# PEER gather kernel: v rows of token block 0 gathered by token and summed on TensorE, in turn with the u rows of block 1

## The chip, the cores and the metric

One core of one Trainium2 chip runs the whole program. The metric is the device time of one execution in microseconds, as the median of several runs. A profiled execution is one such run with the hardware profiler on; its trace gives the start and end of every instruction, and the span from the first to the last instruction.

## The reference

One layer of an encoder on 1024 tokens of width 1024: RMSNorm, a projection, differential attention (4 heads) beside spatial gating (4 groups), an output projection with a residual, then the PEER step below with a residual, and a last RMSNorm. PEER scores each token against two sets of 128 keys for each of 8 heads, keeps 16 experts of 16384 for each head, and sums their v rows with gated weights:

```python
def peer(xn, w_q, sub_keys, w_u, w_v):
    ...
    def block(xb):                       # 128 tokens
        q = (xb @ w_q).reshape(PEER_TOKEN_BLOCK, PEER_HEADS, 2, PEER_HALF)
        s = jnp.einsum('thpd,hpnd->thpn', q, sub_keys).astype(jnp.float32)
        vals, idx = lax.top_k(s, K)
        ...
        expert = i1 * PEER_KEYS + i2
        g = jax.nn.softmax(best, axis=-1)
        h = jnp.einsum('thkd,td->thk', w_u[expert], xb)
        a = (g * jax.nn.gelu(h.astype(jnp.float32))).astype(xb.dtype)
        return jnp.einsum('thk,thkd->td', a, w_v[expert])
```

So each token has 8 x 16 = 128 pairs; a pair needs one row of `w_u` (1024 floats, 4 KB) for a dot product with the token, and one row of `w_v` to be added with weight `a`.

## The kernel before

The 1024 tokens are 8 blocks of 128. The program has a front (`front()`), in which attention, gating, projections and the choice of experts run in four passes of two blocks each, and after it the PEER sums, done in two ways:

- **Dense blocks** (2 to 5, `dense()`): TensorE goes over all 16384 experts in 128 steps. Each step streams 128 u columns and 128 v rows (512 KB each) through the SP queue, ScalarE and VectorE split them into high and low parts (`uh`, `ul`, `vh`, `vl`, lines 760 to 779), and TensorE does `hp` (lines 765 to 767) and the products into `y` and `op` (lines 743 to 745). The gates `gg` that say which token uses which expert are made in the front by `gates()` from one-hot products (`oh`, `pgg`, `st`; lines 598 to 652) and go through the DRAM array `gd`.
- **Gather blocks** (0, 1, 6, 7): `gather_u(b)` fetches, for each of the 128 pairs j, one u row for each of the 128 tokens, by an indirect DMA on GpSimd's queue (line 664, 128 rows of 4 KB, 512 KB), and VectorE forms the dot product (line 685). `gather_v(b)` fetches v rows in the same way, and VectorE adds each with its weight to `y` (line 699). That is 1024 indirect DMAs in all, named `u` and `v` in the trace. They land in a ring of `GAT` = 5 buffers (pool `gat`); once the front has closed its pools, the gathers in `MIXED` have `GAT2` = 3 more.

The order in which the program is written is `PLAN` for the front, then `SEQ`. Letters: A projection, B attention, M gating, Y and D output projection and residual, S scores and top-16 per key set, t the choice of experts (`select`), u and v gathers, G1 and G2 the gates of blocks 2, 3 and 4, 5. A scheduler then orders each engine's instructions by a timing of its own: an instruction goes where its operands and buffers are free, earlier text having priority, and a tile of a pool waits for its turn at the pool's buffers. On the chip each engine runs its own list in that order. So `u1` and `v0`, which stand behind `d` (dense) in `SEQ`, were in fact placed among the front's instructions: they need only `gat` buffers, GpSimd and VectorE.

PSUM has 8 banks. In the front, pool `accp` has 4, `smp` 3 (attention, transposes, G2's gates) and `vpsp` 1 (the gates of G1, alone). `dense()` takes all 8, six for `kept` and two for `hp`.

The call of G1's gates, and the SEQ loop:

```python
                elif w == "G1":
                    gates(G1B, vpsp, "vps", G1)
...
        for w in SEQ.split():
            if w == "d":
                dense()
            else:
                (gather_u if w[0] == "u" else gather_v)(int(w[1:]))
```

Of the kernel before, what the change touches and what calls it, by code (L numbers as in the profile page):

```python
# [7 lines left out]
F32 = mybir.dt.float32  # L8
F32R = mybir.dt.float32r
BF16 = mybir.dt.bfloat16  # L10
I32 = mybir.dt.int32
U32 = mybir.dt.uint32
AF = mybir.ActivationFunctionType
ALU = mybir.AluOpType
AX = mybir.AxisListType
PSUM = bass.MemoryType.PSUM
# [26 lines left out]
FRONT_POOL = 1.0  # L43
WS = 3
G1B = (2, 3)
G1 = dict(st=1, o1=2, o2=3, gt=1)
G2 = dict(st=3, o1=4, o2=4, gt=2)
PLAN = "A0:34 A0:01g2 B0 Y0 D0 S0 X t0 u0 t1 A1:34201 A2:20134 M1 B1 Y1 D1 S1 A3:01234 B2 M2 t2 t3 Y2 M3 D2 B3 S2 t4 t5 G1 Y3 Z G2 D3 S3"
SEQ = "d u1 v0 v1 u6 v6 u7 v7"
LATE = {2: 6, 6: 7}  # L50
GAT = 5
GAT2 = 3
# [9 lines left out]
def peer_block(tc, d):  # L62
# [3 lines left out]
    with ExitStack() as ctx:  # L66
# [65 lines left out]

        x1_d = [dram.tile([P, D], F32, name=f"x1_{b}") for b in range(NB)]
        gd = dram.tile([P, NTB, P, TB], F32, name="gd")
        xT_d = dram.tile([P, DC, TD], F32, name="xT_d")
        sel_t = {}
        rs2_t = {}
# [91 lines left out]
        def front():  # L229
# [1 line left out]
            E2 = fs.enter_context  # L231
            accp = E2(tc.tile_pool(name="accp", bufs=4, space=PSUM))
            smp = E2(tc.tile_pool(name="smp", bufs=3, space=PSUM))
            vpsp = E2(tc.tile_pool(name="vpsp", bufs=1, space=PSUM))
            kv = E2(tc.tile_pool(name="kv", bufs=1))
            sm = E2(tc.tile_pool(name="small", bufs=4))
            tpool = E2(tc.tile_pool(name="tp", bufs=2))
            wp = E2(tc.tile_pool(name="wp", bufs=WP))
            f2 = E2(tc.tile_pool(name="f2", bufs=2))
            f4 = E2(tc.tile_pool(name="f4", bufs=X4))  # L240
            space["sel"] = E2(tc.tile_pool(name="f1", bufs=1))

            gmix = col(kv, "g_mix", DC)
# [336 lines left out]
            for w in PLAN.split():  # L580
                if w == "X":
                    wss.close()
                elif w == "Z":
                    att.close()
                elif w == "G1":
                    gates(G1B, vpsp, "vps", G1)
                elif w == "G2":
                    gates([b for b in DENSE if b not in G1B], smp, "smp", G2)
                elif w[0] in "uvt":
                    {"u": gather_u, "v": gather_v, "t": select}[w[0]](int(w[1:]))  # L590
                elif w[0] == "A":
# [65 lines left out]
        def fetch(b, src, ix, nm):  # L657
            k_ = ring[0] % (GAT + GAT2)
            ring[0] += 1
            if f"{src[2]}{b}" in MIXED and k_ >= GAT:  # L660
                t = gat2.tile([P, D], F32, name=f"{nm}", tag="gat2")
            else:
                t = gat.tile([P, D], F32, name=f"{nm}", tag="gat")
            pool.indirect_dma_start(out=t, out_offset=None, in_=d[src],  # L664
                                    in_offset=bass.IndirectOffsetOnAxis(ap=ix, axis=0))
            return t

        G = {}

        def gather_u(b):  # L670

            n = NPAIR
            ef, _, g = sel_t[b]
            idx = gxn.tile([P, n], I32, name=f"idx{b}", tag="idx", bufs=2)
            dve.tensor_copy(idx, ef)
            xn = gxn.tile([P, D], F32, name=f"xn{b}", tag="xn")
            x1 = gat.tile([P, D], F32, name=f"gx1{b}", tag="gat")
            pool.dma_start(x1, x1_d[b])
            gr = gat.tile([P, D], F32, name=f"gr{b}", tag="gat")
            pool.dma_start(gr, d["g_ffn_row"].partition_broadcast(P))  # L680
            dve.scalar_tensor_tensor(xn, x1, rs2_t[b], gr, op0=ALU.mult, op1=ALU.mult)
            h = gxn.tile([P, n], F32, name=f"h{b}", tag="h")
            for j in range(n):
                t = fetch(b, "w_u", idx[:, j:j + 1], f"u{b}_{j}")
                dve.tensor_tensor_reduce(t, t, xn, 1.0, 0.0, ALU.mult, ALU.add, h[:, j:j + 1])  # L685
            a = gxn.tile([P, n], F32, name=f"a{b}", tag="a")
            act.activation(a, h, AF.Gelu_apprx_tanh)
            dve.tensor_tensor(a, a, g, ALU.mult)
            G[b] = a, idx

        def gather_v(b):

            n = NPAIR
            a, idx = G[b]
            y = gxn.tile([P, D], F32, name=f"y{b}", tag="xn")
            pool.dma_start(y, x1_d[b])
            for j in range(n):
                t = fetch(b, "w_v", idx[:, j:j + 1], f"v{b}_{j}")
                dve.scalar_tensor_tensor(y, t, a[:, j:j + 1], y, op0=ALU.mult, op1=ALU.add)  # L699
            ms = smg.tile([P, 2], F32, name=f"msg_{b}", tag="msg")  # L700
            jk = gxn.tile([P, D], BF16, name=f"jk3_{b}", tag="jk", bufs=1)
            act.activation(jk, y, AF.Square, accum_out=ms[:, 0:1])
            r = rsqrt(ms[:, 0:1], 1, 1.0 / D, f"rl{b}", smg)
            gf = gat.tile([P, D], F32, name=f"gf{b}", tag="gat")
# [165 lines left out]
```

## Time and profile before

| | |
|---|---|
| median of 3 runs | 2812.53 us (2807.18 to 2818.32) |
| the profiled execution | 2825.71 us, its span 2823.9 us |
| granted TensorE clock, mean | 0.91 of full speed |
| busy: TensorE, VectorE | 2423.6 us (86%), 2404.8 us (85%) |
| busy: ScalarE, GpSimd | 1000.3 us (35%), 1488.8 us (53%) |
| indirect gathers (software queue) | 545.33 MB, 53.0% of the 16 DMA engines' time |

How to read it: a share is a mean over stages with different limits, so the stages are read one by one, by time windows. A window's line gives the busy time of each engine in it. "Idle before" is the time in which an engine stood still ahead of an instruction, and behind the arrow is what ended that wait. fp32 matmuls leave two records in the trace for each call.

### The profile page before, as it was taken

Reading aid. Unit: us, or ns where it says so; the run is one execution under the profiler, and the core shown is the slowest. Engines: PE = TensorE matmul, PEld = TensorE weight load, DVE = VectorE, ACT = ScalarE, POOL = GpSimd, SP = SyncE. Lnnn points to the kernel's source line nnn. Section 1 sums busy time; section 2 is a strip of 40 time slices with the busy share of each in tenths; the row PEclk is TensorE's granted clock in tenths of the full one; section 3 lists DMA queues with packets and bytes.
Section 4 is the critical chain, followed back from the end, with each engine's and each line's share of the span. In section 5 each row is a group of like instructions: output and inputs, shape, how many; then the busy total and the mean of one; then the engine's idle time right before and its main releaser. Section 6 shows DMA issues by size and latency. Waiting matters only on the chain.

```text
span 2823.9 us, 33571 instructions
## 1 busy us (share of the span) xinstructions
PE 2423.6 (86%) x10764; PEld 1909.5 (68%) x10764; DVE 2404.8 (85%) x5223; ACT 1000.3 (35%) x2063; POOL 1488.8 (53%) x1139
## 2 busy tenths in 40 slices
PE   6789997995569774797999999999999999999930
PEld 5575655753447542695887887888888888888820
DVE  4448867999988999999898887987888978888998
ACT  5553322224553542983323232232232322323300
POOL 5362564356655325321265646655566657655665
PEclk9799998996569777898999999999999999999965
DMA  5266999998899858797699999999999989998998
GB/s 174 59 181 184 343 365 359 337 339 297 299 348 331 295 182 290 264 366 247 214 346 350 352 322 366 354 333 342 328 356 343 342 306 384 349 359 303 331 333 343
DMA packets 316514, 869.56 MB, mean 308 GB/s; under 512 B 26033, under 2 KB 93745, under 8 KB 312241
## 3 DMA queue, kind: packets, MB, share of 16 engines
q0 software_dynamic: 149760, 545.33, 53.0%
q1 hardware_dynamic: 166576, 322.09, 33.2%
q8 instruction: 85, 1.39, 0.2%
q14 instruction: 93, 0.75, 0.1%
HBM read 823.28 MB, written 44.04 MB: 307 GB/s over the span
## 4 chain that ended last, share of the span: by engine, by line
PE 61%; DVE 19%; DMA 10%; issue 5%; ACT 4%; POOL 1%; SPq 0%; DVEq 0%; ACTq 0%; POOLq 0%
PE hp L765 7%; PE hp L767 7%; PE hp L766 7%; PE y L745 6%; PE y L743 6%; PE y L744 6%; PE pq L309 5%; DVE y L699 4%; DVE u L685 4%; DMA u<-in_w_u_dram,idx 3%; PE pgg L650 2%; PE wi L309 2%; PE op L743 2%; PE op L745 2%; PE op L744 2%
## 5 line engine op out<-in xcount | busy, mean ns | idle before, releaser
L664 POOL DMA_INDIRECT v<-in_w_v_dram,idx x512 | 664.9, 1299 | 656.5 <-DVE y L699 321.2
L664 POOL DMA_INDIRECT u<-in_w_u_dram,idx x512 | 700.1, 1367 | 530.7 <-DVE h L685 226.7
L699 DVE SCALAR_TENSOR_TENSOR y<-v,a,y 128x1024 f32<-128x1024 f32 x512 | 656.3, 1282 | 15.8 <-DMA v<-in_w_v_dram,idx 9.0
L685 DVE CUSTOM_DVE_ANT_0 u<-u,xn 128x1024 f32<-128x1024 f32 x512 | 614.2, 1220 | 50.6 <-DMA u<-in_w_u_dram,idx 50.2
L765 PE MATMUL hp<-xh,uh 128*128 128x512 f32 x1024 | 400.0, 391 | 22.0 <-ACT xh L726 15.6
L766 PE MATMUL hp<-xl,uh 128*128 128x512 f32 x1024 | 399.3, 390 | 2.4 <-DVE xl L727 2.4
L767 PE MATMUL hp<-xh,ul 128*128 128x512 f32 x1024 | 399.3, 390 | 0.6 <-DVE ul L761 0.6
L778 ACT ACTIVATE vh<-vr 128x1024 fp32r<-128x1024 f32 x128 | 130.7, 1052 | 510.8 <-PE op L745 481.1
L744 PE MATMUL y<-vl,ah 128*128 128x512 f32 x768 | 298.8, 389 | 0.0
L743 PE MATMUL y<-vh,ah 128*128 128x512 f32 x768 | 298.8, 389 | 0.0
L745 PE MATMUL y<-vh,al 128*128 128x512 f32 x768 | 287.6, 389 | 2.2 <-DVE al L775 2.2
L650 PE MATMUL pgg<-oh,oh 128*128 128x128 f32 x1024 | 190.3, 344 | 102.7 <-ACT st L651 63.9
L650 PEld LDWEIGHTS pgg<-oh,oh 128*128 128x128 f32 x1024 | 170.3, 247 | 132.6 <-ACT st L651 84.0
L765 PEld LDWEIGHTS hp<-xh,uh 128*128 128x128 f32 x1024 | 192.7, 188 | 64.4 <-ACT xh L726 15.8
L766 PEld LDWEIGHTS hp<-xl,uh 128*128 128x128 f32 x1024 | 192.7, 188 | 43.0 <-DVE xl L727 3.1
L767 PEld LDWEIGHTS hp<-xh,ul 128*128 128x128 f32 x1024 | 192.6, 188 | 41.4 <-DVE ul L761 1.4
L760 ACT ACTIVATE uh<-ur 128x1024 fp32r<-128x1024 f32 x128 | 135.1, 1056 | 168.7 <-PE hp L766 149.7
L761 DVE TENSOR_TENSOR ul<-ur,uh 128x1024 fp32r<-128x1024 f32 x128 | 156.3, 1221 | 36.6 <-ACT uh L760 36.5
L309 PE MATMUL pq<-sT,sc 128*128 128x256 f32 x768 | 184.0, 389 | 0.7 <-ACT sT L127 0.7
L779 DVE TENSOR_TENSOR vl<-vr,vh 128x1024 fp32r<-128x1024 f32 x128 | 153.5, 1220 | 16.3 <-ACT vh L778 16.3
L745 PEld LDWEIGHTS y<-vh,al 128*128 128x128 f32 x768 | 144.2, 188 | 33.3 <-DVE al L775 3.5
L309 PEld LDWEIGHTS pq<-sT,sc 128*128 128x128 f32 x768 | 143.8, 195 | 32.8 <-issue 10.7
(440 smaller groups left out, 4117.2 us busy)
## 6 DMA issues: line engine op xcount, KB each, us to landing
ur<-in_w_uT_dram SPq DMA_DIRECT2D x128, 512.0 KB, 6.5
vr<-in_w_v_dram SPq DMA_DIRECT2D x128, 512.0 KB, 6.5
wi<-in_w_in_dram SPq DMA_DIRECT2D x80, 512.0 KB, 5.0
sc<-in_w_q_dram SPq DMA_DIRECT2D x64, 512.0 KB, 6.4
gd<-st SPq DMA_DIRECT2D x32, 1024.0 KB, 7.2
gg<-gd SPq DMA_DIRECT2D x16, 2048.0 KB, 21.8
wo<-in_w_out_dram SPq DMA_DIRECT2D x32, 512.0 KB, 7.0
x<-in_x_dram SPq DMA_DIRECT2D x16, 512.0 KB, 6.5
```

The source lines that it names most:

```text
L309: pe.matmul(ps, s_[i], m_[j], start=first and n == 0, stop=last and n == len(ops) - 1, **kw)
L650: pe.matmul(pg[:, j * P:(j + 1) * P], oh2[:, j, :], oh1[:, j, :], start=True, stop=True)
L664: pool.indirect_dma_start(out=t, out_offset=None, in_=d[src], in_offset=bass.IndirectOffsetOnAxis(ap=ix, axis=0))
L685: dve.tensor_tensor_reduce(t, t, xn, 1.0, 0.0, ALU.mult, ALU.add, h[:, j:j + 1])
L699: dve.scalar_tensor_tensor(y, t, a[:, j:j + 1], y, op0=ALU.mult, op1=ALU.add)
L743: pe.matmul(ps, ah[:, bs], vh[:, hs], start=first, stop=False, skip_group_check=True)
L744: pe.matmul(ps, ah[:, bs], vl[:, hs], start=False, stop=False, skip_group_check=True)
L745: pe.matmul(ps, al[:, bs], vh[:, hs], start=False, stop=last, skip_group_check=True)
L761: dve.tensor_tensor(ul, ur, uh, ALU.subtract)
L765: pe.matmul(hp[:, :TD], uh[:, ds_], xh[:, dc, :], start=(dc == 0), stop=False)
L766: pe.matmul(hp[:, :TD], uh[:, ds_], xl[:, dc, :], start=False, stop=False)
L767: pe.matmul(hp[:, :TD], ul[:, ds_], xh[:, dc, :], start=False, stop=(dc == DC - 1))
```

## The change

Block 0's v sum leaves VectorE. `tokens_v` turns the expert numbers and the weights `a` by a transpose, so that a gather fetches for one token its 128 rows (one pair on each partition). A matmul with a 128x32 weight matrix, zero but for one column that holds the token's `a`, adds the sum over pairs to one row of a PSUM tile; the column moves over 32 places, and the four 32-column groups of the array take two tokens by two halves of the row. Each of 64 steps (2 halves `r`, 32 `j`) has two gathers and four fp32 matmuls of 512 columns. `both` interleaves this with the u rows of block 1, in turn, as the last item `w01` of `PLAN`; `u1` and `v0` leave `SEQ`. G1's gates now share `smp` in place of the bank `vpsp`, which `vyp` takes for the sums, and have one `oh1` buffer fewer.

```diff
-G1 = dict(st=1, o1=2, o2=3, gt=1)
+G1 = dict(st=1, o1=2, o2=2, gt=1)
...
-PLAN = "A0:34 A0:01g2 B0 Y0 D0 S0 X t0 u0 t1 A1:34201 A2:20134 M1 B1 Y1 D1 S1 A3:01234 B2 M2 t2 t3 Y2 M3 D2 B3 S2 t4 t5 G1 Y3 Z G2 D3 S3"
-SEQ = "d u1 v0 v1 u6 v6 u7 v7"
+PLAN = "A0:34 A0:01g2 B0 Y0 D0 S0 X t0 u0 t1 A1:34201 A2:20134 M1 B1 Y1 D1 S1 A3:01234 B2 M2 t2 t3 Y2 M3 D2 B3 S2 t4 t5 G1 Y3 Z G2 D3 S3 w01"
+SEQ = "d v1 u6 v6 u7 v7"
+TENSOR = [0]
+VJ = 1
...
-            vpsp = E2(tc.tile_pool(name="vpsp", bufs=1, space=PSUM))
+            vyp = E2(tc.tile_pool(name="vyp", bufs=1, space=PSUM))
...
+            sv = E2(tc.tile_pool(name="sv", bufs=1))
...
-                    gates(G1B, vpsp, "vps", G1)
+                    gates(G1B, smp, "smp", G1)
...
+                elif w[0] == "w":
+                    both(int(w[1]), int(w[2]), smp, vyp, sv)
...
+        def tokens_v(b, pp, vyp, sv):
...
+            ef = sel_t[b][0]
+            pt = pp.tile([P, 512], F32, name=f"vt{b}", tag="smp")
+            pe.transpose(pt[:, 0:P], ef, ident)
+            pe.transpose(pt[:, P:2 * P], G[b][0], ident)
+            ixT = sv.tile([P, P], I32, name=f"ixT{b}", tag="ixT")
+            aT = sv.tile([P, P], F32, name=f"aT_{b}", tag="aTv")
+            act.activation(ixT, pt[:, 0:P], AF.Copy)
+            act.activation(aT, pt[:, P:2 * P], AF.Copy)
+            W = [sv.tile([P, 2, VJ, 63], F32, name=f"vw{b}_{i}", tag=f"vw{i}") for i in range(2)]
+            for w_ in W:
+                dve.memset(w_, 0.0)
+            for r in range(2):
+                ps = vyp.tile([P, 512], F32, name=f"vy{b}_{r}", tag="vy")
+                for j in range(32):
+                    w_ = W[j // VJ % 2]
+                    if j % VJ == 0:
+                        act.activation(w_[:, :, :, 31], aT[:, r * 64:r * 64 + 64].rearrange("p (g j) -> p g j", g=2)[:, :, j:j + VJ], AF.Copy)
+                    vs = [fetch(b, "w_v", ixT[:, r * 64 + g * 32 + j:r * 64 + g * 32 + j + 1], f"v{b}_{r}_{j}_{g}") for g in range(2)]
+                    for hf in range(2):
+                        for g in range(2):
+                            q0 = 64 * hf + 32 * g
+                            pe.matmul(ps[q0:q0 + 32, :], w_[:, g, j % VJ, 31 - j:63 - j], vs[g][:, hf * 512:(hf + 1) * 512],
+                                      start=(j == 0), stop=(j == 31), tile_position=(0, q0), skip_group_check=True)
+                    yield
+                    yield
+                y2 = gat.tile([P, D], F32, name=f"vs{b}_{r}", tag="gat")[:, 0:512]
...
+                dve.tensor_tensor(y2, y2, ps, ALU.add)
+                for hf in range(2):
+                    pool.dma_start(yv_d[b][r * 64:(r + 1) * 64, hf * 512:(hf + 1) * 512], y2[64 * hf:64 * hf + 64, :])
+            y = gxn.tile([P, D], F32, name=f"y{b}", tag="xn")
+            pool.dma_start(y, yv_d[b])
+            finish_v(b, y)
...
+        def both(bv, bu, pp, vyp, sv):
...
+            todo = [rows_u(bu), tokens_v(bv, pp, vyp, sv)]
+            while todo:
+                for g_ in list(todo):
+                    if next(g_, 0) == 0:
+                        todo.remove(g_)
```

`rows_u` is the old `gather_u` with a `yield` behind each row, and `finish_v` the old end of `gather_v` (the last norm and the store of the block).

What the scheduler made of it shows in the lists of the engines. Three places follow.

TensorE, the gates of block 2 (`gt2` are their transposes, `pgg` their products; `ops5` and `ops7` are the attention sums of blocks 5 and 7). Before:

```order
L477 MATMUL ops5_4810<-v4_174,aT5_3_4_4941 128x128
L477 MATMUL ops5_4810<-v5_175,aT5_3_4_4941 128x128
L611 MATMUL gt2_1_6559<-ident_75,rj2_5148 128x128
L611 MATMUL gt2_2_6562<-ident_75,g2_5153 128x128
L650 MATMUL pgg0_0_6576<-oh1_0_0_6568,oh2_0_0_6567 128x128 x4
L650 MATMUL pgg0_4_6591<-oh1_0_4_6583,oh2_0_4_6582 128x128 x4
```

Now:

```order
L481 MATMUL ops7_5753<-v7_181,aT7_3_4_5898 128x128
L125 MATMUL mT7ap0_5931<-ident_75,mix7_5751 128x128
L617 MATMUL gt2_0_6560<-ident_75,ri2_5144 128x128
L125 MATMUL mT7ap0_5931<-ident_75,mix7_5751 128x128 x3
L617 MATMUL gt2_1_6563<-ident_75,rj2_5152 128x128
L617 MATMUL gt2_2_6566<-ident_75,g2_5157 128x128
L313 MATMUL wo3_0_7_8622<-wo3_0_0_8623,mT3_5485 128x512 x2
L313 MATMUL wo3_0_7_8622<-wo3_0_1_8629,mT3_5485 128x512 x2
L656 MATMUL pgg0_0_6580<-oh1_0_0_6572,oh2_0_0_6571 128x128 x4
```

The gates of blocks 2 and 3 stood between the attention of block 5 and that of block 6; now they stand behind the attention of block 7, the last one.

TensorE, the end of the front (`ss` are the last scores, `hp` the first products of the dense stage). Before:

```order
L559 MATMUL ss6_3_9100<-kt3_3_8995,sq3_3_9039 128x128 x2
L559 MATMUL ss7_3_9129<-kt3_3_8995,sq3_3_9039 128x128 x2
L765 MATMUL hp0_9229<-xh_9189,uh0_9225 128x512
L765 MATMUL hp1_9271<-xh_9189,uh1_9267 128x512
L766 MATMUL hp0_9229<-xl_9190,uh0_9225 128x512
```

Now:

```order
L656 MATMUL pgg31_8_8594<-oh1_31_8_8586,oh2_31_8_8585 128x128 x3
L656 MATMUL pgg31_12_8609<-oh1_31_12_8601,oh2_31_12_8600 128x128 x4
L708 MATMUL vt0_9174<-ident_75,ri0_2372 128x128
L709 MATMUL vt0_9174<-ident_75,a0_2786 128x128
L727 MATMUL vy0_0_9185<-v0_0_0_0_9187,vw0_0_9181 32x512
L727 MATMUL vy0_0_9185<-v0_0_0_1_9189,vw0_0_9181 32x512
L727 MATMUL vy0_0_9185<-v0_0_0_0_9187,vw0_0_9181 32x512
L727 MATMUL vy0_0_9185<-v0_0_0_1_9189,vw0_0_9181 32x512
L727 MATMUL vy0_0_9185<-v0_0_1_0_9202,vw0_1_9182 32x512
```

and 250 matmuls further on:

```order
L727 MATMUL vy0_1_9672<-v0_1_31_0_10139,vw0_1_9182 32x512
L727 MATMUL vy0_1_9672<-v0_1_31_1_10141,vw0_1_9182 32x512
L828 MATMUL hp0_10255<-xh_10215,uh0_10251 128x512
L828 MATMUL hp1_10297<-xh_10215,uh1_10293 128x512
L829 MATMUL hp0_10255<-xl_10216,uh0_10251 128x512
```

All 256 matmuls of the new sum (`vy`) stand in a row, behind the last gate and ahead of the first `hp`.

GpSimd, behind the last u row of block 0 (`dio` is the index row for the gates of G2). Before:

```order
L664 DMA u0_127_2779<-in_w_u_dram,idx0_2389 128x1024
L678 DMA gx11_18114<-x1_1_87 128x1024
L680 DMA gr1_18116<-in_g_ffn_row_dram 128x1024
L664 DMA u1_0_18120<-in_w_u_dram,idx1_18111 128x1024
L664 DMA u1_1_18123<-in_w_u_dram,idx1_18111 128x1024
L664 DMA u1_2_18126<-in_w_u_dram,idx1_18111 128x1024
```

The rest of `u1` follows there in a row, and `v0` behind it.

Now:

```order
L670 DMA u0_127_2783<-in_w_u_dram,idx0_2393 128x1024
L684 DMA gx11_9165<-x1_1_87 128x1024
L686 DMA gr1_9167<-in_g_ffn_row_dram 128x1024
L670 DMA u1_0_9171<-in_w_u_dram,idx1_9162 128x1024
L610 IOTA dio_7598 128x128
L670 DMA v0_0_0_0_9187<-in_w_v_dram,ixT0_9177 128x1024
L670 DMA v0_0_0_1_9189<-in_w_v_dram,ixT0_9177 128x1024
L670 DMA u1_1_9195<-in_w_u_dram,idx1_9162 128x1024
L670 DMA u1_2_9198<-in_w_u_dram,idx1_9162 128x1024
L670 DMA v0_0_1_0_9202<-in_w_v_dram,ixT0_9177 128x1024
```

Behind the first u row of block 1 GpSimd now has the index row of G2 and two v rows that need the transposed indices `ixT`; the rest alternates, two u rows and two v rows.

## Rows read from the trace of the kernel before

**Rows 1.** The page: span, busy time of each engine and its share of the span.

```profile
span 2823.9 us, 33571 instructions
PE 2423.6 (86%) x10764; PEld 1909.5 (68%) x10764; DVE 2404.8 (85%) x5223; ACT 1000.3 (35%) x2063; POOL 1488.8 (53%) x1139
```

**Rows 2.** Time windows (start:end, length, then busy us of each engine, clock, DMA, GB/s).

```profile
core 0: us, PE busy (x) PEld busy (x) DVE busy (x) ACT busy (x) POOL busy (x), PEclk, DMA share, GB/s
560.00:650.00 90.00, 87.24 (x296) 51.06 (x295) 90.00 (x368) 20.93 (x45) 49.10 (x39) 0.98 0.94 331
650.00:1085.00 435.00, 288.99 (x1239) 215.08 (x1239) 400.15 (x1140) 196.95 (x542) 218.72 (x176) 0.72 0.83 291
1085.00:1297.00 212.00, 168.52 (x921) 139.75 (x920) 205.65 (x597) 144.01 (x379) 68.16 (x54) 0.89 0.89 311
1297.00:2707.00 1410.00, 1398.32 (x6144) 1153.24 (x6143) 1224.06 (x1642) 409.91 (x527) 813.22 (x577) 1.00 0.92 331
960.00:1040.00 80.00, 62.83 (x249) 43.14 (x249) 72.58 (x236) 43.66 (x109) 19.75 (x21) 0.69 0.64 211
```

**Rows 3.** All gathers of u and of v: duration min/median/max ns, first and last start.

```profile
L664 POOL DMA_INDIRECT u<-in_w_u_dram,idx x512: 932/1346/4157, 270.7 to 2566.9; - x171
L664 POOL DMA_INDIRECT v<-in_w_v_dram,idx x512: 932/1020/3759, 852.6 to 2805.8; - x171
```

**Rows 4.** Dense matmuls: `hp` first start, `op` last start, the page's line on `hp`.

```profile
L765 PE MATMUL hp<-xh,uh x1024: 387/389/792, 1296.6 to 2687.2; 128*128 128x512 f32 x171
L745 PE MATMUL op<-vh,al x256: 388/389/389, 1342.9 to 2706.5; 128*128 128x512 f32 x128
L765 PE MATMUL hp<-xh,uh 128*128 128x512 f32 x1024 | 400.0, 391 | 22.0 <-ACT xh L726 15.6
```

**Rows 5.** VectorE by line, 565 to 1297 us (busy us, mean ns | idle before).

```profile
L699 DVE SCALAR_TENSOR_TENSOR y<-v,a,y 128x1024 f32<-128x1024 f32 x129 | 165.1, 1280 | 2.7 <-DMA v<-in_w_v_dram,idx 2.3
L685 DVE CUSTOM_DVE_ANT_0 u<-u,xn 128x1024 f32<-128x1024 f32 x130 | 156.9, 1218 | 14.8 <-DMA u<-in_w_u_dram,idx 14.8
```

**Rows 6.** TensorE by line, 650 to 1085 us.

```profile
L650 PE MATMUL pgg<-oh,oh 128*128 128x128 f32 x512 | 113.5, 388 | 84.4 <-ACT st L651 62.1 <-DVE oh L641 14.1 <-ACT oh L646 3.7
L309 PE MATMUL pq<-sT,sc 128*128 128x256 f32 x256 | 60.7, 385 | 0.0
```

**Rows 7.** TensorE by line, 1085 to 1297 us.

```profile
L650 PE MATMUL pgg<-oh,oh 128*128 128x128 f32 x512 | 76.8, 300 | 18.4 <-DVE oh L641 8.3 <-ACT oh L645 4.7 <-ACT oh L646 3.5
L309 PE MATMUL pq<-sT,sc 128*128 128x256 f32 x256 | 62.4, 387 | 0.7 <-ACT sT L127 0.7
```

**Rows 8.** ScalarE by line, 565 to 1297 us.

```profile
L646 ACT ACTIVATE oh<-oh,gT 128x128 f32<-128x128 f32 x256 | 111.7, 491 | 11.1 <-DVE gT L613 11.1
L645 ACT ACTIVATE oh<-iota,gT 128x128 f32<-128x128 f32 x256 | 89.1, 402 | 11.8 <-PE pgg L650 11.7
L651 ACT ACTIVATE st<-pgg 128x512 f32<-128x512 f32 x128 | 76.2, 596 | 94.1 <-PE pgg L650 67.0 <-DMA gd<-st 26.9
```

**Rows 9.** Tile `gd`, 960 to 1045 us: gate stores, five of them, issue to landing.

```profile
DMA to landing us min/median/max: 3.8/5.4/7.2
```

**Rows 10.** Tile `v`, 960 to 1040 us: gathers under light DMA load, issue to landing.

```profile
L664 POOL DMA_INDIRECT v<-in_w_v_dram,idx x21: 936/937/1003, 960.9 to 1037.1; - x21
DMA to landing us min/median/max: 4.1/4.6/6.6
```

**Rows 11.** TensorE, fp32 matmuls of 512 columns in a row, 565 to 1297 us.

```profile
L309 PE MATMUL wi<-wi,xT 128*128 128x512 f32 x96 | 43.0, 598 | 0.0
```

**Rows 12.** Timeline of GpSimd in the tail, gathers of v7 alone (start, duration, engine).

```profile
2768.78 1.02 POOL L664 DMA_INDIRECT v<-in_w_v_dram,idx  x1 [0.30 <-issue]
2770.10 1.01 POOL L664 DMA_INDIRECT v<-in_w_v_dram,idx  x1 [0.30 <-issue]
```

**Rows 13.** Gathers of v at the start of the dense stage and 100 us later.

```profile
L664 POOL DMA_INDIRECT v<-in_w_v_dram,idx x14: 936/1138/3759, 1298.2 to 1398.8; - x14
L664 POOL DMA_INDIRECT v<-in_w_v_dram,idx x47: 933/1144/1993, 1400.0 to 1496.1; - x47
```

More of the change, by code (lines that the diff above doesn't have):

```diff
@@ L134, in peer_block @@
         gd = dram.tile([P, NTB, P, TB], F32, name="gd")
+        yv_d = {b: dram.tile([P, D], F32, name=f"yv_{b}") for b in TENSOR}
         xT_d = dram.tile([P, DC, TD], F32, name="xT_d")
@@ L668, in peer_block, with rows_u @@
         G = {}
-        def gather_u(b):
+        def rows_u(b):
             n = NPAIR
@@ L689, in gather_u @@
             G[b] = a, idx
+        def gather_u(b):
+            for _ in rows_u(b):
+                pass
+        def tokens_v(b, pp, vyp, sv):
[23 more added lines that the diff above has]
+                    yield
+                    yield
+                y2 = gat.tile([P, D], F32, name=f"vs{b}_{r}", tag="gat")[:, 0:512]
+                rows = x1_d[b][r * 64:(r + 1) * 64, :]
+                for hf in range(2):
+                    pool.dma_start(y2[64 * hf:64 * hf + 64, :], rows[:, hf * 512:(hf + 1) * 512])
+                dve.tensor_tensor(y2, y2, ps, ALU.add)
+                for hf in range(2):
+                    pool.dma_start(yv_d[b][r * 64:(r + 1) * 64, hf * 512:(hf + 1) * 512], y2[64 * hf:64 * hf + 64, :])
+            y = gxn.tile([P, D], F32, name=f"y{b}", tag="xn")
+            pool.dma_start(y, yv_d[b])
+            finish_v(b, y)
@@ L699, in gather_v, with finish_v @@
                 dve.scalar_tensor_tensor(y, t, a[:, j:j + 1], y, op0=ALU.mult, op1=ALU.add)
+            finish_v(b, y)
+        def finish_v(b, y):
             ms = smg.tile([P, 2], F32, name=f"msg_{b}", tag="msg")
```

## The prediction

> **What bounds the kernel now.** I read the page first: VectorE 85% and TensorE 86% busy over the span, so neither share alone tells the limit [rows 1]. Then time windows, because the stages differ [rows 2]. In the front from 560 to 1297 us VectorE is busy for 90.0 of 90, 400.2 of 435 and 205.7 of 212 us, TensorE for 87.2, 289.0 and 168.5: behind 650 us VectorE is the limit and TensorE's clock falls to 0.72 for want of work. From 1297 to 2707 us TensorE is busy for 1398 of 1410 us at clock 1.00: the dense stage is bound by TensorE, from its first `hp` at 1296.6 to its last `op` at 2706.5 [rows 4]. Then the gathers of block 7 go on alone: the last v gather is issued at 2805.8 [rows 3], and the span ends at 2823.9. So the end is set by the stream of gathers, which runs from 270.7 to 2805.8 without a long break, 1024 of them at a mean of (2805.8 - 270.7) / 1023 = 2.48 us; and the dense stage runs beside it and ends 117 us earlier.
>
> What counts for the change is therefore: when does the dense stage start, and how many gathers are left at that moment. Before, at 1297 us, all of u0, u1 and v0 are done (384 gathers) and 640 are left. After the change the same 384 must be done before the first `hp`, because TensorE's list has all `vy` matmuls ahead of it. From there the same 640 gathers and the same dense work remain. The new time is the new start of the dense stage plus about what follows it now, 2823.9 - 1296.6 = 1527 us.
>
> **Part 1: what leaves VectorE.** The 128 v additions of block 0 (mean 1.28 us) are about 164 us, and 128 u rows of block 1 (1.22 us and a short read of the sum) about 157 us move out of the front's middle to its end [rows 5]. Both were spent in the front, where VectorE was the limit. They are a gain only as far as the front really gets shorter.
>
> **Part 2: the front without them.** GpSimd's list is unchanged up to the first u row of block 1. The 256 u gathers of blocks 0 and 1 lie between 270.7 and the first v at 852.6, 2.27 us each, so the 129th is at about 561 us [rows 3]. Until 650 us TensorE is full (87.2 of 90) and nothing is won. Then the order of the gates decides. Since G1's gates now share `smp`, they wait for their turn behind the attention of block 7. What is left of 650 to 1085 us without gates is TensorE's 289.0 - 113.5 = 176 us [rows 2, 6]; to this I add an estimated 45 us, a quarter, for chains of norm and transpose that nothing fills (in the window behind it TensorE idles 43.5 us beside 168.5 of work [rows 2]): attention ends at about 871 us. G1 then has 16 chunks of 16 tokens with a single `st` buffer. ScalarE needs for one chunk 4 copies of 76.2 / 128 = 0.60 us, 8 first steps of 89.1 / 256 = 0.35 and 8 second steps of 111.7 / 256 = 0.44, in sum 8.7 us [rows 8]; about 2.7 us of it (six one-hot steps) stand in its list ahead of the first copy of the next chunk and so run while the store of the last chunk lands, which takes 3.8 to 7.2, median 5.4 us under light load [rows 9]. A chunk is 5.4 + 6.0 = 11.4 us, 16 of them 182 us (157 to 211). G1 ends at 1053 us. Behind it come the second half of D3, S3 and G2: TensorE has 168.5 us in the window that holds them now, 76.8 of it G2's gates and 62.4 the scores [rows 2, 7], VectorE 205.7 less some 50 for v0. I take 172 us: 1225. The two transposes, the copies to `ixT` and `aT` and the first landing of a v row (4.6) are 8 us more: the first `vy` at 1233 us (1195 to 1275). So the front, up to there, is only some 48 us shorter than its 1281 us now (1296.6 less the wait of 15.6 for `xh` [rows 4]): the 320 us that left VectorE are given back to waits, as the gates were hidden beside attention and the gathers, and now stand alone. GpSimd does next to nothing from 565 to 1225 us: the ring of five is held by `u1_0` to `u1_2` and the first two v rows, which need `ixT`.
>
> **Part 3: the pair of sums.** Now 256 gathers run with five buffers and little beside them. A buffer is used again five gathers later, and four gathers make a step (two u, two v), so the second v row of a step takes the buffer of the first v row of the step before. It cannot be issued until TensorE is done with that row, and TensorE cannot go on until it has landed. The period of a step is that loop: issue to landing 4.6 us under light load (4.1 to 6.6) [rows 10]; then two more matmuls until the first row is free (the first of the four needs only the first row and is done already); then two hand-overs between queues, an estimated 0.6 us (twice the 0.30 that stands between gathers [rows 12]). An fp32 matmul of 512 columns is two records of 43.0 / 96 = 0.45 us, so 0.9 us at a granted clock of 0.98 and 1.8 us at half of it [rows 2, 11]; no row of this trace has a matmul of 32 columns. Bounds for two of them: 0.9 us (side by side, full clock) to 3.6 us (one behind the other, half clock). I take 1.8. The period is 4.6 + 1.8 + 0.6 = 7.0 us, 64 steps 448 us. GpSimd's own pace, 1.32 us from one gather to the next [rows 12], would allow 5.3 us a step, and VectorE's two u rows 2.6 us: both are hidden. I add an estimated 30 us: two periods at the turn from the first half to the second (GpSimd's queue waits for the addition of 64 rows), and a third of the 50 us that the selects of blocks 6 and 7 take (Part 4), since ScalarE's weights stand behind them in its list. TensorE leaves the sums at 1233 + 478 = 1711 us.
>
> The Trainium skill, page "TensorE: Matmul & The Clock Gate", section "Part 3: Packing small matmuls", says that matmuls on different column groups run at the same time, and gives 2.38 times for three tiles of 32 columns and 512 columns of data. By that rule the two matmuls cost 0.9 to 1.8 us, not up to 3.6, and the sum would be that of rival B or mine. No run here shows it yet.
>
> **Part 4: the dense stage and the tail.** `xh` is made behind the last u row, and TensorE waits for it as now: 15 us, so the first `hp` is at 1726 us. Of the 1527 us that follow now, some come back: in the first 100 us GpSimd issues 14 gathers, in the next 47 [rows 13]. The gap of 33 gathers at 2.1 us is 70 us of a VectorE full with the choice of experts for blocks 6 and 7 and the first splits. The selects now run beside the sums, where VectorE has room; I take 50 us back (0 to 70). The end is 1726 + 1477 = 3203 us of span. The profiled execution stands 1.8 us above its span and 13.2 us above the median (2825.71 against 2812.53), so the forecast is 3203 + 1.8 - 13.2 = **3192 us**, 13% slower.
>
> Hidden at no cost: the extra stores and loads of `yv` (they lie beside the first dense products), ScalarE's 64 small copies of weights (a step ahead), the memsets.
>
> **Rivals.**
> - B, quick sums: the matmuls of a step go side by side at full clock, two cost 0.9 us, and the period is 6.1 us or less, down to GpSimd's 5.3. Then the sums take 338 to 390 us instead of 448, and the time is 3082 to 3134. For it: four different column groups. Against: TensorE would be idle for most of a step, and in the window from 960 to 1040 us, with more work than that, the clock was 0.69.
> - C, slow sums: matmuls one behind the other at half clock, a period of 8.8 us, 115 us more: 3307. Or gathers come no faster than u rows did with the same five buffers, 2.27 us each, 581 us instead of 448: 3325. For it: that was the pace in the front. Against: 0.94 busy DMA engines there, which would be much less here.
> - D, faster: the front was bound by VectorE, and shrinks by all of 322 us, to 959; the sums go at GpSimd's pace, 256 x 1.32 = 338 us; dense starts at 959 + 338 + 15 = 1312, the span ends at 1312 + 1477 = 2789, the time is 2778, 1.2% faster. It decides if the sums end before about 1320 us. Against: TensorE alone has 545 us of work from 560 to 1297, and the gates stand behind attention in its list.
> - E, no change: halfway between, the sums end at about 1330 us. It needs nearly all that D needs.
>
> That the change doesn't do what it says is not among them: the additions are gone from VectorE's list.
>
> **How the numbers follow.** Forecast 50%, B 24%, C 21%, D 3%, E 2%. The range reaches over B's lower end with a front at its early bound, and over C: 3060 to 3330 us. About 0.5%, 14 us, is what a measurement can tell from no change: faster 0.03, same 0.02, slower 0.95.
>
> **What would show it.** In the profile after: GpSimd nearly idle from about 565 to 1225 us; the first `vy` at 1195 to 1275; 64 steps of 6 to 9 us, with TensorE waiting for DMA of v and GpSimd waiting for TensorE; the first `hp` right behind the last `vy`; from there to the end some 1480 us, with the tail of block 7 behind TensorE as now. I would be wrong if gates ran well before 871 us, if the gathers of `u1` filled the gap, or if the stage behind the first `hp` were shorter than 1410 us.

## The result, and the profile after

The changed kernel takes 3164.4 us against 2813.5 us: a ratio of 1.1237, with a 95% interval from 1.120 to 1.1275, so 12% slower. One of its four executions was in a slower state (3782.2 us at a granted clock of 0.683); the ratio leaves it out, the median has it in. The profiled execution has a span of 3153.2 us (before 2823.9).

Time windows of the kernel after; columns as in [rows 2].

```profile
560.00:650.00 90.00, 82.35 (x291) 47.28 (x289) 68.13 (x322) 22.86 (x58) 0.37 (x1) 1.00 0.41 125
650.00:880.00 230.00, 194.47 (x771) 127.62 (x771) 146.16 (x718) 82.40 (x241) 0.00 (x0) 0.85 0.28 85
880.00:1085.00 205.00, 163.97 (x936) 137.18 (x936) 116.86 (x307) 185.24 (x505) 0.23 (x1) 0.92 0.41 156
1085.00:1235.00 150.00, 88.75 (x493) 60.23 (x491) 133.73 (x574) 63.19 (x171) 41.66 (x35) 0.76 0.74 259
1235.00:1670.00 435.00, 215.41 (x496) 31.61 (x496) 149.09 (x242) 20.95 (x69) 269.18 (x238) 0.58 0.84 284
1670.00:3060.00 1390.00, 1384.54 (x6095) 1144.70 (x6094) 1195.94 (x1453) 399.35 (x515) 814.24 (x592) 1.00 0.94 339
```

From 650 to 1085 us VectorE, the limit there before, is busy for 263 of 435 us (before 400 [rows 2]), and GpSimd for a quarter of a microsecond. From 1235 to 1670 us there is a stage that the kernel before does not have: TensorE is half busy at a clock of 0.58, and no engine is full (the DMA engines stand at 0.84). Behind it the dense stage is what it was: 1405 us from the first `hp` to the last `op`, before 1410.

The tiles of gates, v sums and dense products in the kernel after: count, duration of one in ns (least, median, most), first and last start in us, shape. They answer to [rows 4, 6, 7].

```profile
L656 PE MATMUL pgg<-oh,oh x1024: 272/275/582, 859.7 to 1145.2; 128*128 128x128 f32 x171
...
L727 PE MATMUL vy<-v,vw x512: 589/1061/1063, 1153.7 to 1650.4; 128*32 128x512 f32 x171
...
L828 PE MATMUL hp<-xh,uh x1024: 389/389/796, 1655.8 to 3040.2; 128*128 128x512 f32 x171
```

The gates run from 860 to 1145 us, behind the attention and no longer beside it; the sums from 1154 to 1651; `hp` follows 4.4 us after the end of the last `vy`. The difference of the spans, 329 us, comes out of these rows: the front up to the first `vy` is 142.9 us shorter than the front up to the first `hp` was (1153.7 against 1296.6), sums and their hand-over add 502.1, and from the first `hp` to the end it takes 1497.4 us instead of 1527.3, which is 29.9 back. About 25 of these lie behind the last `op`, where the remaining gathers take 93 us instead of 117.

GpSimd's list in the kernel after around its long pause (start, us, instruction, and in brackets how long the engine stood idle before it and what ended that).

```profile
559.38 0.99 POOL L670 DMA_INDIRECT u<-in_w_u_dram,idx  x1 [2.03 <-DVE rep L571]
995.62 0.23 POOL L610 IOTA dio<- 128x128 int32 x1 [435.25 <-PE mT7bp L125]
1146.52 0.97 POOL L670 DMA_INDIRECT v<-in_w_v_dram,ixT  x1 [150.67 <-ACT aT L713]
```

GpSimd works through its list in order: the `iota` of G2's gates waits until the last transpose of block 7 is done, and behind it the first v row waits for `aT`, since the sums stand last in `PLAN`. So from 650 to 1085 us, where the DMA engines are busy for only 0.28 to 0.41 of the time, no gather is issued.

### The profile page after: what moved, and what is told of

The parts are those of the page before. It is cut to its first block, busy times and chain, and to the rows that moved or that the text cites. A ratio compares the mean times of both kernels' runs of the same rounds, so it can differ in the third digit from the quotient of the medians.

```text
span 3153.2 us, 34803 instructions
## 1 busy us (share of the span) xinstructions
PE 2614.2 (83%) x11278; PEld 1903.2 (60%) x11278; DVE 2280.0 (72%) x5099; ACT 1002.4 (32%) x2125; POOL 1453.0 (46%) x1147
## 3 DMA queue, kind: packets, MB, share of 16 engines
q1 hardware_dynamic: 166576, 322.09, 29.9%
## 4 chain that ended last, share of the span: by engine, by line
PE 62%; DVE 11%; issue 10%; POOL 6%; DMA 5%; ACT 4%; SPq 0%; another core or an unknown queue 0%; POOLq 0%; DVEq 0%; ACTq 0%
PE hp L828 7%; PE hp L829 7%; PE hp L830 7%; PE pq L313 6%; PE y L806 5%; PE y L807 5%; PE y L808 5%; PE wi L313 3%; POOL u L670 3%; PE wo L313 3%; DVE y L758 3%; POOL v L670 2%; PE qk L313 2%; PE pgg L656 2%; PE s L448 2%
## 5 line engine op out<-in xcount | busy, mean ns | idle before, releaser
L670 POOL DMA_INDIRECT u<-in_w_u_dram,idx x512 | 677.1, 1323 | 479.3 <-DVE h L691 227.2
L670 POOL DMA_INDIRECT v<-in_w_v_dram,idx x384 | 509.2, 1326 | 358.3 <-DVE y L758 250.3
L758 DVE SCALAR_TENSOR_TENSOR y<-v,a,y 128x1024 f32<-128x1024 f32 x384 | 492.2, 1282 | 12.0 <-DMA y<-x 4.2
L727 PE MATMUL vy<-v,vw 128*32 128x512 f32 x512 | 229.5, 1031 | 276.3 <-DMA v<-in_w_v_dram,ixT 267.7
L727 PEld LDWEIGHTS vy<-v,vw 128*32 128x32 f32 x512 | 23.7, 139 | 480.6 <-issue 355.4
L670 POOL DMA_INDIRECT v<-in_w_v_dram,ixT x128 | 138.3, 1080 | 283.4 <-ACT aT L713 150.7
L656 PE MATMUL pgg<-oh,oh 128*128 128x128 f32 x1024 | 159.1, 301 | 40.0 <-DVE oh L647 19.4
```

The costliest lines, as they stand in the source:

```text
L656: pe.matmul(pg[:, j * P:(j + 1) * P], oh2[:, j, :], oh1[:, j, :], start=True, stop=True)
L727: pe.matmul(ps[q0:q0 + 32, :], w_[:, g, j % VJ, 31 - j:63 - j], vs[g][:, hf * 512:(hf + 1) * 512], start=(j == 0), stop=(j == 31), tile_po ...
```

## One step of the sums

A step of 64 in the kernel after, all engines' lines that belong to the loop (columns as above).

```profile
1300.64 0.94 POOL L670 DMA_INDIRECT v<-in_w_v_dram,ixT  x1 [1.60 <-PE vy L727]
...
1303.65 1.52 PE L727 MATMUL vy<-v,vw 128*32 128x512 f32 x2 [3.28 <-DMA v<-in_w_v_dram,ixT]
1304.55 0.93 POOL L670 DMA_INDIRECT v<-in_w_v_dram,ixT  x1 [0.30 <-issue]
...
1305.81 1.85 PE L727 MATMUL vy<-v,vw 128*32 128x512 f32 x6 [0.63 <-DMA v<-in_w_v_dram,ixT]
1307.81 0.21 ACT L722 ACTIVATE vw<-aT 128x2 f32<-128x2 f32 x1 [7.09 <-PE vy L727]
1307.94 0.94 POOL L670 DMA_INDIRECT v<-in_w_v_dram,ixT  x1 [2.45 <-PE vy L727]
```

The second v row of a step is issued at 1300.64, its three matmuls start at 1305.81 and end at 1307.66, and at 1307.94 GpSimd issues the second v row of the next step into the buffer that the matmuls have freed. Over all 64 steps the medians are 5.27 us from issue to these matmuls, 1.93 us for the matmuls and 0.28 us to the next issue: 7.48, and the median step, from first matmul to first matmul, is 7.43. Who waits in that stage says the same (engine, what, for whom: us in total, times, longest):

```profile
PE vy L727 <- DMA v<-in_w_v_dram,ixT: 267.7, 98, 21.7
DVE u L691 <- DMA u<-in_w_u_dram,idx: 241.3, 94, 5.9
...
POOL v L670 <- PE vy L727: 108.1, 57, 3.9
```

TensorE waits for the landing, GpSimd for TensorE: a circle, in which from 1235 to 1670 us TensorE is busy for only 215 of 435 us and GpSimd for 269. The DMA engines, at 0.84, have the least to spare; whether they or the ring of five buffers set the step is what the run with eight buffers below decides.

## Experiments

Ratios are to the kernel before, with 95% intervals.

**Sums moved early** (`e1_sums_early`):

```
- PLAN = "... A3:01234 B2 M2 t2 t3 ... Z G2 D3 S3 w01"
+ PLAN = "... A3:01234 B2 w01 M2 t2 t3 ... Z G2 D3 S3"
```

> Only the place of w01 in PLAN differs from the changed kernel: it stands ahead of M2 instead of behind S3, so vt gets its turn at smp before the attention of blocks 6 and 7 and TensorE's list has the vy matmuls among attention, gates and scores. Theory A (the loss is the place: 497 us of sums stand alone between the front and the dense stage, while GpSimd rested from 565 to 1147 us): the sums now run beside the front from about 670 us at 7.5 us a step, the first hp follows the front at 1230 to 1350 us, and with 1497 us behind it the time is 2730 to 2850 us, no slower than before. Rival B (the sums by token are dear wherever they stand, since TensorE waits in order for each pair of rows and holds up what is behind it): the front grows by most of what is saved, first hp at 1500 us or later, time 3000 us or more.

2861.6 us, 1.0127 [1.008, 1.0174]: 303 us below the kernel after, by one word moved. So the place of the sums is nearly all of the loss. Its tiles:

```profile
L727 PE MATMUL vy<-v,vw x512: 589/617/1063, 666.2 to 1304.5; 128*32 128x512 f32 x171
L656 PE MATMUL pgg<-oh,oh x1024: 272/275/582, 947.1 to 1310.8; 128*128 128x128 f32 x171
L828 PE MATMUL hp<-xh,uh x1024: 389/389/795, 1342.0 to 2728.9; 128*128 128x512 f32 x171
```

The sums take longer, 638 us, but beside the front, and mostly at the high level of the clock (median record 617 ns instead of 1061; the granted clock from 666 to 1305 us is 0.91). Yet the first `hp` is at 1342, not 1297, and the kernel is not faster than before; theory A's 2730 to 2850 us was 12 us too good.

**u rows of block 1 apart** (`e2_u1_apart`):

```
- PLAN = "... S2 t4 t5 G1 Y3 Z G2 D3 S3 w01"
+ PLAN = "... S2 u1 t4 t5 G1 Y3 Z G2 D3 S3 w0"
...
- both(int(w[1]), int(w[2]), smp, vyp, sv)
+ [None for _ in tokens_v(int(w[1:]), smp, vyp, sv)]
```

> The changed kernel with u1 taken out of the pair: block 1's u rows are gathered ahead of t4 in PLAN (so among the front's work, as before), and only block 0's v rows are summed at the end (two gathers a step). Theory A (the pair's step is the loop of five buffers, landing plus two matmuls plus hand-over, 7.5 us for four gathers): with two gathers a step the five buffers hold two and a half steps, the period is 3.0 us (7.5 / 2.5), between TensorE's own 1.9 and GpSimd's 2.6 us for two gathers and the full 7.5; the sums take 64 x 3.0 + 20 = 210 us instead of 497, the front grows by up to 40 us, time 2870 to 2930 us. Rival B (a gather by token costs what a gather costs in the pair, 7.5 / 4 = 1.9 us, set by DMA): 64 x 3.8 = 240 us plus the turn, 2910 to 2960 us. Rival C (a step costs 7.5 us however many gathers it has): 480 us, no gain, 3150 us.

2992.7 us, 1.062 [1.0583, 1.0658], above what theories A and B gave and far below C.

```profile
L727 PE MATMUL vy<-v,vw x512: 589/617/1064, 1234.7 to 1483.5; 128*32 128x512 f32 x171
```

The v rows alone take 249 us, with a median step of 3.42 us. So C fell, but the run does not decide between A (a step of 3.0, 210 us) and B (3.8, 240 us and the turn): the step lies between them, the total nearer to B. And the first `vy` is 81 us later than in the kernel after, twice the cost that was allowed: the u rows are again work for VectorE in the front; that this work is what delays it was not separated.

**Eight buffers** (`e3_eight_buffers`):

```
+ space["g3"] = E2(tc.tile_pool(name="gather3", bufs=3))
...
+ if nm[:2] in ("u1", "v0"):
+     k_ = ring[1] = (ring[1] + 1) % (GAT + 3)
```

> The changed kernel with eight buffers instead of five for u1 and v0: three more open where the attention's pools close (Z). Nothing else differs. Theory A (loop through the buffers): a row's buffer comes back two steps later instead of one, the loop no longer binds, the step falls from 7.5 us to GpSimd's pace, 4 x 1.32 = 5.3 us, or a little more; the sums fall from 497 to about 370 us, the time to 3030 to 3050 us. Rival B (DMA or TensorE at half clock sets the step): less than 20 us are won, 3145 us or more.

3062.2 us, 1.0854 [1.0818, 1.089]: 102 us below the kernel after.

```profile
L732 PE MATMUL vy<-v,vw x512: 589/1061/1064, 1162.9 to 1545.9; 128*32 128x512 f32 x171
```

The sums take 383 us instead of 497, with a median step of 5.97. Nothing but the number of buffers changed, so the ring of five did set the step. GpSimd's wait for TensorE, 108.1 us above, has all but gone:

```profile
POOL v L675 <- PE vy L732: 10.6, 7, 4.0
```

The step does not come down to the 5.3 that theory A named, and the time is 12 us above its range. From 1163 to 1546 us the DMA engines are busy for 0.96 of the time and move 357 GB/s, where the kernel after has 0.86 and 292 in the same window, and the landing is slower (median 6.36 us from issue to the matmuls instead of 5.27). So with eight buffers the DMA engines are the next limit, and GpSimd's pace is out of reach.

**Half the columns** (`e8_half_columns`): `vy` matmuls of 256 columns instead of 512; the other half of the columns is left out.

```
- pe.matmul(ps[q0:q0 + 32, :], ..., vs[g][:, hf * 512:(hf + 1) * 512], ...
+ pe.matmul(ps[q0:q0 + 32, 0:256], ..., vs[g][:, hf * 512:hf * 512 + 256], ...
```

> The kernel after with vy matmuls of 256 columns instead of 512; it leaves out half of the columns of block 0's v sum. Gathers, buffers, order and waits are the same. Theory A (a step is a loop of landing, two matmuls and a hand-over through the five buffers): the matmuls of a step take 0.9 us instead of 1.85, the step 6.5 us instead of 7.4, the sums 60 us less: 3095 to 3115 us. Rival B (the step is set by GpSimd's issue or by what the DMA engines move, and the matmuls are hidden): 3155 to 3170 us.

3128.1 us, 1.1103 [1.1065, 1.1141]: 36 us below the kernel after, between the two theories. One step of it:

```profile
1299.87 0.94 POOL L670 DMA_INDIRECT v<-in_w_v_dram,ixT  x1 [1.52 <-PE vy L727]
...
1305.15 1.07 PE L727 MATMUL vy<-v,vw 128*32 128x256 f32 x6 [0.63 <-DMA v<-in_w_v_dram,ixT]
1306.36 0.21 ACT L722 ACTIVATE vw<-aT 128x2 f32<-128x2 f32 x1 [6.42 <-PE vy L727]
1306.50 0.94 POOL L670 DMA_INDIRECT v<-in_w_v_dram,ixT  x1 [1.00 <-PE vy L727]
```

The matmuls take 1.07 us instead of 1.93 (medians), 0.86 less. From one issue of the second v row to the next, the median step falls from 7.40 to 6.70 us, by 0.70. So the matmuls do lie in the loop, which rival B denied. Over all 63 loops they save 50 us, and some 33 of these remain: about 9 come back in slower landings and about 9 in later issues, 6 of the latter in the one long wait that both kernels have while VectorE chooses experts (23.3 us instead of 17.4).

**Only the gates moved** (`e4_g1_on_smp`), in the kernel before:

```
- gates(G1B, vpsp, "vps", G1)
+ gates(G1B, smp, "smp", G1)
```

> The kernel before with one part of the change alone: G1's gates on smp instead of their own bank, with two oh1 buffers instead of three. u1 and v0 are gathered and summed on VectorE as before. Theory A (the gates move behind the attention of block 7, as in the changed kernel, but the front is limited by VectorE and the gathers fill it, so a new order of the same work moves little): first hp at 1290 to 1340 us, time 2800 to 2860 us. Rival B (what the gates hid beside attention is lost as soon as they stand alone, some 130 us of gates): first hp at 1400 us or later, time 2920 us or more.

2866.5 us, 1.0173 [1.0137, 1.0209]. The gates in the kernel before and in this run, and this run's `hp`:

```profile
L650 PE MATMUL pgg<-oh,oh x1024: 272/275/583, 670.9 to 1259.3; 128*128 128x128 f32 x171
```

```profile
L650 PE MATMUL pgg<-oh,oh x1024: 272/275/582, 997.8 to 1309.5; 128*128 128x128 f32 x171
L765 PE MATMUL hp<-xh,uh x1024: 389/389/792, 1338.2 to 2726.7; 128*128 128x512 f32 x171
```

The first gate comes at 998 us instead of 671, the first `hp` at 1338 instead of 1297. So this part of the change alone costs some 50 us, about as much as `e1_sums_early` still lost.

**A bank for the gates again.** That suggested to give G1 a bank back, taken from the accumulators (`e5_early_own_bank`) or from the small tiles (`e6_early_two_smp`), with a control for the bank in the kernel before (`e7_before_three_acc`).

```
- accp = E2(tc.tile_pool(name="accp", bufs=4, space=PSUM))
+ accp = E2(tc.tile_pool(name="accp", bufs=3, space=PSUM))
+ vpsp = E2(tc.tile_pool(name="vpsp", bufs=1, space=PSUM))
...
- gates(G1B, smp, "smp", G1)
+ gates(G1B, vpsp, "vps", G1)
```

> The sums placed early as in e1_sums_early, and the gates of G1 put back on a PSUM bank of their own, which the stage's accumulators give up (three banks instead of four). Theory A: what e1_sums_early still lost against the kernel before (some 45 us) is what moving G1 to the shared banks cost (some 50 us in e4_g1_on_smp). Then the first hp comes at about 1297 us as before and the time is 2800 to 2830 us, ratio 0.995 to 1.005. Rival B: the loss comes from the sums' own steps on TensorE (stalls of in-order vy matmuls that wait for a landing with attention queued behind them); the bank changes nothing: 2850 to 2870 us, first hp at about 1340.

> As e5_early_own_bank, but the bank for G1 is taken from the shared small tiles (two banks instead of three), and the accumulators keep four. Theory A: 2800 to 2850 us, later than e5_early_own_bank if the transposes of the front need three banks, earlier if the accumulators need four. Rival B: 2850 to 2880 us.

> The kernel before with three accumulator banks instead of four and nothing else: the price of the bank that e5_early_own_bank gives up. Theory A: the dense stage is bound by TensorE at clock 1.00 and three banks are enough: within 10 us of the kernel before. Rival: the accumulators wait for their eviction, 1 to 2 per cent slower (2840 to 2870 us), and then this and not the sums is what e5_early_own_bank would lose.

2858.1 us (1.0146 [1.0113, 1.0179]), 2876.4 us (1.0218 [1.0185, 1.025]) and, for the control, 2842.9 us (1.0099 [1.0067, 1.0132]). Theory A fell in the first two: the bank brings nothing on balance. The control says one half of why: the bank itself costs some 30 us, in the range that the control's rival gave, and most of it in the front (first `hp` at 1318.0 against 1296.6). That accumulators wait for their eviction, as the rival had it, was not looked into.

```profile
L765 PE MATMUL hp<-xh,uh x1024: 387/389/794, 1318.0 to 2704.5; 128*128 128x512 f32 x171
```

The tiles of `e5_early_own_bank` say the other half:

```profile
L657 PE MATMUL pgg<-oh,oh x1024: 272/275/583, 650.2 to 1226.1; 128*128 128x128 f32 x171
L728 PE MATMUL vy<-v,vw x512: 592/617/1064, 692.9 to 1359.9; 128*32 128x512 f32 x171
L829 PE MATMUL hp<-xh,uh x1024: 389/389/794, 1365.3 to 2744.7; 128*128 128x512 f32 x171
```

The gates no longer end the front; the sums do, which began at 693 although the u rows of block 0 were done at 565 and GpSimd was idle from 564 to 689.

**Earlier still.** The sums stand ahead of `B2`; with the bank for G1 (`e9_earlier_own_bank`), with G1 on the small tiles (`e10_earlier_shared_banks`), and with G1 on the accumulators (`e11_earlier_gates_on_acc`).

```
- PLAN = "... A3:01234 B2 M2 t2 t3 ... Z G2 D3 S3 w01"
+ PLAN = "... A3:01234 w01 B2 M2 t2 t3 ... Z G2 D3 S3"
```

> As e5_early_own_bank (bank of its own for G1, three accumulator banks), but the sums stand one stage earlier, ahead of B2, so that the transposes of the indices come soon after the first sum of u rows ends (565 us) and not at 687. Theory A: in e5_early_own_bank the front's end is the gathers' end (690 to 1353 us, 2.6 us each, behind them the first hp at 1365), so 70 to 100 us that GpSimd idles are won: first hp at 1280 to 1310, time 2780 to 2810 us, level with the kernel before or better. Rival B: TensorE, 85 to 90 per cent busy from 650 to 1300 us with the vy matmuls added, is the bound; an earlier start only spreads the gathers, first hp at 1340 to 1365, time 2840 to 2865 us.

> As e1_sums_early (G1 on the shared banks, four accumulators), with the sums one stage earlier, ahead of B2. Theory A: there the sums ended at 1305 and the gates of G1 at 1311 us, both late; an earlier start frees only the sums, the gates still wait for their turn behind block 7's attention: first hp at 1320 to 1345, time 2840 to 2865 us. Rival B: the sums held the gates back, since both need TensorE and ScalarE: first hp at 1280 to 1300, time 2800 to 2820 us.

> As e10_earlier_shared_banks, but G1 takes its turn on the four accumulator banks, so that no bank is given up and the gates stand behind the q and key products and not behind block 7's attention tiles. Theory A (what is lost is the gates' place in the order): gates start before 1000 us, first hp at 1270 to 1300, time 2770 to 2810 us, level with or below the kernel before. Rival B (TensorE's work is the bound, or output products wait for accumulators that gates hold): 2830 to 2870 us.

The first gives 2821.6 us, 1.002 [1.0002, 1.0037], 0.2% above the kernel before, whose level theory A had named; its 2780 to 2810 us was 12 us too good, its first `hp` (1299.6) was right, and rival B fell. It is the best place found.

```profile
L728 PE MATMUL vy<-v,vw x512: 589/617/1064, 583.2 to 1251.2; 128*32 128x512 f32 x171
L829 PE MATMUL hp<-xh,uh x1024: 388/389/794, 1299.6 to 2684.6; 128*128 128x512 f32 x171
```

Against the control with the same three accumulators, `e7_before_three_acc`, it is 21 us shorter. That is less than 1%, but the two intervals, each against the kernel before, do not touch. So the idea in itself, well placed, is worth about 21 us by this comparison, and the bank that it takes costs about 30. The window from 650 to 1300 us in it and then in the control (columns as in [rows 2]) shows what was exchanged:

```profile
650.00:1300.00 650.00, 569.42 (x2731) 346.58 (x2730) 480.78 (x1619) 357.34 (x992) 267.21 (x245) 0.93 0.88 311
```

```profile
650.00:1300.00 650.00, 469.64 (x2247) 357.58 (x2245) 606.15 (x1742) 343.44 (x929) 275.99 (x226) 0.82 0.82 290
```

VectorE has 125 us less, TensorE 100 us more. VectorE was the busiest engine with 606 of 650 us; now TensorE is, with 569, and the DMA engines stand at 0.88. The other two confirm that the gates' place must come with it: 2866.4 us (1.0183 [1.0157, 1.0209]), with sums that end at 1177 and gates at 1315, as theory A said (1.4 us above its range); and 2851.9 us (1.0118 [1.009, 1.0145]), where theory A fell and rival B was right: the gates start at 897 and end at 1273, but the products `pq` of blocks 6 and 7 take their turn on the accumulators behind them and run until 1325.

```profile
L656 PE MATMUL pgg<-oh,oh x1024: 272/275/583, 897.4 to 1273.3; 128*128 128x128 f32 x171
L313 PE MATMUL pq<-sT,sc x256: 379/379/792, 1232.4 to 1325.0; 128*128 128x256 f32 x128
```

**Late sums, but a bank for the gates** (`e12_late_own_bank`): the edit of `e5_early_own_bank` in the kernel after.

> The sums stay where the change puts them (behind everything else of the front), only the gates of G1 get a bank of their own back, which the accumulators give up (three instead of four). Theory A (Part 2 of the prediction: in the kernel after G1's gates stand alone behind block 7's attention, 136 us from 860 to 996): with the bank they run beside attention again, the first vy comes at 1020 to 1060 us instead of 1154, the sums are as long as in the kernel after (480 to 500 us), and the time is 3040 to 3090 us. Rival B (the front is bound by TensorE and by the chains of attention, so that the gates' place does not matter): first vy at 1130 to 1170, time 3150 to 3190 us.

3122.3 us, 1.1088 [1.1055, 1.112]: between the theories, 42 us below the kernel after.

```profile
650.00:880.00 230.00, 214.53 (x1011) 148.23 (x1010) 134.62 (x602) 128.01 (x359) 0.00 (x0) 0.97 0.37 119
880.00:1085.00 205.00, 180.35 (x1049) 155.36 (x1049) 165.04 (x605) 181.85 (x502) 0.23 (x1) 0.89 0.45 167
...
L728 PE MATMUL vy<-v,vw x512: 589/1061/1064, 1113.3 to 1611.6; 128*32 128x512 f32 x171
```

With gates from 650 us on, the first `vy` comes only 40 us earlier, at 1113, and TensorE is busy for 395 of the 435 us. From 560 to 1106 us it is busy for 491 of 546, so at its granted clock of 0.92 no order of this work could bring more than some 55 us: with VectorE relieved, TensorE is the front's next limit, close behind. The run also gives up the accumulator bank that cost the front some 21 us in `e7_before_three_acc`, so the place of the gates may be worth more than the 40 us seen; no run separates the two.

## Why the prediction was right, and where it was not

The forecast was 3192 us, 28 us above the result and well inside the range. The sign and the mechanism hold: the sums stand between front and dense stage, the front gives back less than they cost, and the step is the loop through five buffers (`e3_eight_buffers`, `e8_half_columns`). The two largest misses of single terms lie in the stages of the gates.

- **End of attention.** Said 871 us; the first gate starts at 859.7. GpSimd is idle from 560 to 1147 (said 1225).
- **G1's gates, mis-sized.** Said 182 us, with 5.4 us of each chunk for a store that nothing hides. Measured 136 (860.8 to 996.5), 8.5 us a chunk. ScalarE is busy for 118 of these 136 us, so its own work nearly fills the chunk (the 8.7 of the prediction adds durations that overlap a little). In that stretch it waits for the store once:

```profile
ACT st L657 <- PE pgg L656: 13.8, 5, 7.5
...
ACT st L657 <- DMA gd<-st: 1.1, 1, 1.1
```

  The work of the next chunk that needs no `st` just covers the store: between the last copy of a chunk and the first of the next ScalarE does 13 one-hot steps (median), which keep it busy for 4.5 us, where the prediction counted six and 2.7 us.
- **G2, scores and the rest.** Said 172 us, measured 150.
- **First `vy`.** Said 1233 (1195 to 1275), measured 1153.7: outside its bounds, by the two terms above. Part 2 also blamed the gates' place for the whole of what was given back; `e12_late_own_bank`, at the price of a bank, got 40 us back by it, and TensorE's own work, 491 of 546 us there, limits what more there is to get. Rival D's counter-argument, TensorE's 545 us of work, had it right. Nor was it the ring that kept GpSimd idle, as Part 2 has it: only `u1_0` was issued ahead of the pause, and `u1_1` stands in GpSimd's list behind two v rows that wait for `ixT`.
- **The step.** Said 4.6 + 1.8 + 0.6 = 7.0 us; measured 5.3 + 1.9 + 0.3 = 7.5. The landing was undersized: the 4.6 came from a window with the DMA engines at 0.64 [rows 2, 10], and the pair's own traffic keeps them at 0.84. The hand-over was oversized. Sums said 478 us, measured 497. Rivals B (quick sums) and C (sums with matmuls one behind the other) fell: the three matmuls of different column groups do run side by side, at the low level of the clock; and the second form of C, gathers at 2.27 us each, came out at 1.94 (497 us for 256). The stall of the selects was there, but not where it was put, at ScalarE's weights:

```profile
1190.17 1.68 POOL L670 DMA_INDIRECT u<-in_w_u_dram,idx  x1 [21.56 <-DVE h L691]
```

  The u rows waited in VectorE's list behind a select and behind a split `ul` of the dense stage, for which VectorE stood idle for 4.7 us; so GpSimd had no buffer for 21.6 us, and TensorE no row for 21.7.
- **Behind the first `hp`.** Said 1477 us, measured 1497: 30 us came back, not 50. The gap of [rows 13] narrowed, from 14 gathers in the first 100 us to 35, but block 1's v rows then met the turn from sums to dense stage: GpSimd's list has waits of 9.5 and 14.5 us for `yv` and `y` there.

```profile
1666.21 0.55 POOL L739 DMA_DIRECT2D y<-yv  x1 [9.53 <-DMA yv<-vs]
...
1682.55 0.97 POOL L670 DMA_INDIRECT v<-in_w_v_dram,idx  x1 [14.49 <-DVE y L769]
```

Front and gates came out 79 us too long, the sums 19 and the tail 20 us too short, the wait for `xh` 10 too long: 79 - 19 - 20 + 10 = 50, the difference between the span of 3203 that was summed and the 3153 measured. So part of the nearness is luck, errors that cancel. That the time is only 28 us off and not 50 is chance too: the prediction took the profiled execution to stand 13 us above the median, as before, and the one after stands 9.5 below it (3154.9 against 3164.4).

What stays open: why some landings and issues came later when the matmuls were halved; why three accumulators cost 21 us in the front; and what the gates' place is worth by itself.

## What to carry to other kernels

Work moved to another engine is worth what its place lets it overlap: the same sums cost 350 us behind the front and, placed beside it with the gates on a bank of their own, some 6 us. Before moving a sum to TensorE, count what it takes besides time, here a PSUM bank and a set of gather buffers. And when streams share a short ring of buffers, look for the loop in it: here four gathers through five buffers took landing plus use plus hand-over, 7.5 us, though GpSimd could have issued them in 5.3, and three more buffers brought the step down to 6.0, with the DMA engines busy for 0.96 of the time.

## What the runs showed of the hardware

Matmuls with 32 columns of weights on different column groups run at the same time. In `e1_sums_early`, at the high level of the clock, one such matmul and then three of them (x2 and x6 records):

```profile
693.21 1.05 PE L727 MATMUL vy<-v,vw 128*32 128x512 f32 x2
...
695.24 1.06 PE L727 MATMUL vy<-v,vw 128*32 128x512 f32 x6
```

Three take 1.06 us, one 1.05; the first records of three start within 14 ns of each other. The Trainium skill, page "TensorE: Matmul & The Clock Gate", section "Part 3: Packing small matmuls", gives 2.38 times for three such tiles with 512 columns of data; here, in fp32, it is 3.0 in these rows, and the measurement decides. The granted clock in the lonely sums was 0.58, with TensorE busy for 215 of 435 us, and the same three took 1.93 us there; beside the front it was 0.93, with TensorE busy for 569 of 650 us (`e9_earlier_own_bank`).
